# Latent up projection: rotary columns of q's weights held twice, rotation of raw values in two operations, k scaled by POOL

## The chip, the cores and the metric

The kernel runs on one core of one Trainium2 chip. A core has TensorE (PE, matrix products; PEld is its weight load), VectorE (DVE), ScalarE (ACT), GpSimd (POOL) and SyncE (SP), which issues the DMAs. Each engine works through its own queue in order; they meet at semaphores. The metric is the device time of one execution in microseconds.

## The reference

One layer of a streaming encoder, 1024 tokens of width 1024: a modulated RMS norm, one input projection, two groups of attention heads (latent attention "MLA" and chunk-band attention "CA"), an output projection, and a gated MLP with a short convolution. What matters here is the latent group, 8 heads of 64 plain and 32 rotary columns:

```python
def rope(x, positions):            # cut
    x1, x2 = xf[..., :half], xf[..., half:]
    out = jnp.concatenate([x1 * cos - x2 * sin, x2 * cos + x1 * sin], axis=-1)
...
q = jnp.dot(rmsnorm(q_lat, g_q_latent[l]), w_q_up[l]).reshape(B, S, MLA_HEADS, MLA_QK)
kv = jnp.dot(rmsnorm(kv_lat, g_kv_latent[l]), w_kv_up[l]).reshape(B, S, MLA_HEADS, MLA_NOPE + MLA_V)
k_nope, v = kv[..., :MLA_NOPE], kv[..., MLA_NOPE:]
k = jnp.concatenate([k_nope, jnp.broadcast_to(k_rope[:, :, None, :], (B, S, MLA_HEADS, MLA_ROPE))], axis=-1)
q = rmsnorm(q, g_mla_q[l])
k = rmsnorm(k, g_mla_k[l])
q = jnp.concatenate([q[..., :MLA_NOPE], rope(q[..., MLA_NOPE:], positions)], axis=-1)
k = jnp.concatenate([k[..., :MLA_NOPE], rope(k[..., MLA_NOPE:], positions)], axis=-1)
o_mla = mla_attention(q, k, v)
```

q is projected from a latent of rank 256, k and v from one of rank 128. Each head's q and k are divided by their root mean square over all 96 columns, and the last 32 columns are rotated by the token's position. The root mean square is one number for a token and head, so scaling and rotation can stand in either order.

## The kernel before, in words

Everything is computed with 128 tokens on the partitions. Products in 32 bits are made of a high and a low part of each operand: `gemm3` (L150) issues three matmuls for each pair, `hi_of` (L75) makes the high part on ACT, `lo_of` (L83) the rest on POOL or DVE.

The stages in order: modulation and norm (to about 70 us), input projection and chunk-band attention (to about 340 us), latent up projection (about 347 to 463 us), latent attention with the output projection of the other head group (to about 612 us), the rest of the output projection and the second norm (to about 710 us), then the MLP.

Attention and projections are woven together: `units` lists the attention units, each with four tiles of 128 queries; after the scores and values of each tile, `pace` takes steps from the list `fillers`, which holds the projections in a fixed order, among them `f_up(0)` and `f_up(1)`. A latent unit of head group 0 needs `f_up(0)` done; one of its second half of queries, `f_up(1)`, since `need` runs a filler to its end. `gemm3_f` yields a cost that depends on the columns of the product, and `pace` counts it.

The order of instructions on each engine is then planned by the framework: it simulates a timeline with modelled costs, scores, softmax and value products have a raised priority (`tc.high_priority`), and `tc.issue_after` pins some instructions behind others.

`f_up(gr)` (L628) handles one group of four heads. It loads q's weights (two pieces of 128 rows, 384 columns: 4 heads of 96) and the shared k and v weights (512 columns), splits them, and goes through the 8 token tiles. For each tile it

- projects q into a PSUM bank `qu` (L661), copies it to a row buffer `uqr` (L664, ACT), squares it (L666, ACT) and sums the squares by head (L669, DVE);
- projects k and v into `ku` (L671), copies k to `kraw` (L675), squares it (L677) and sums (L678); adds the sum of the shared rotary key (L679);
- makes both scales on POOL (`rsqrt_mean`, L119 and L120: a multiply-add and a power to -0.5);
- writes v as a high and a low half (`vt`, L682 on ACT, L683 on DVE);
- scales q into `qn` (L685, DVE) and rotates its rotary columns there with `rope_apply` (L497 to L500, four DVE operations, temporaries in the row buffer);
- scales k into `kn`: plain columns (L689) and the shared, already rotated key `kr` (L690), both on DVE.

Row buffers `uqr` and `kraw` come from one set of four (`rtile`). q and k are later transposed by PE (L729) into pages for the scores (L803). Softmax of a tile is a minimum on DVE (L822), an exponential on ACT (L829), the reciprocal on DVE (L831, L832), a scaling to 16 bits on POOL (L73), its residue on DVE (L851), and a transpose by DMA (L863) ahead of the value products (L891).

`rope_tables` (L539) makes cosine and sine tables times the norm's gains once, early: `tabq` for q and `tabk` for k, 64 columns each: 32 of cosine and 32 of sine (L611).

Of the kernel before, what the change touches and what calls it, by code (L numbers as in the profile page):

```python
# [18 lines left out]
AF = mybir.ActivationFunctionType  # L19
# [3 lines left out]
MUL, ADD, SUB, MIN, MAX = ALU.mult, ALU.add, ALU.subtract, ALU.min, ALU.max  # L23

P = 128
D = 1024
S = 1024
NT = S // P
# [5 lines left out]
QR, KVR, ROPE, NOPE, VD = 256, 128, 32, 64, 64  # L34
QK = NOPE + ROPE
# [29 lines left out]
def layer_kernel(ctx, tc, I, out):  # L65
    nc = tc.nc
    pe, act, dve, pool, sp = nc.tensor, nc.scalar, nc.vector, nc.gpsimd, nc.sync
# [7 lines left out]
    def hi_of(eng, o, i):  # L75
        if eng == "a":
            act.activation(o, i, AF.Copy)  # L77
        elif eng == "p":
            pool.tensor_scalar(o, i, 1.0, 0.0, op0=MUL, op1=ADD)
        else:  # L80
            dve.tensor_copy(o, i)

    def lo_of(eng, o, i, hi):  # L83
        (pool if eng == "p" else dve).tensor_tensor(o, i, f32(hi), op=SUB)  # L84
# [10 lines left out]
    pk = cst.tile([P, C_CV], F32, name="pk")  # L95
# [33 lines left out]
    tabq = apg.tile([P, NT, 64], F32, name="tabq")  # L129
# [409 lines left out]
    def rope_tables():  # L539
        cnt = [0]  # L540

        buf = [pgtile([P, 8, NT, 16], F32, f"rt{i}") for i in range(2)]

        def T():
            n = cnt[0] % 10
            cnt[0] += 1
            return buf[n // 8][:, n % 8]

        keep = (buf[1][:, 6], buf[1][:, 7])

        def rnd(src, q, o=None):
            o = T() if o is None else o
            dve.tensor_scalar(o, src, q, MAGIC, op0=MUL, op1=ADD)
            dve.tensor_scalar(o, o, MAGIC, None, op0=SUB)
            return o

        def fma(n, c, b):
            o = T()
            dve.scalar_tensor_tensor(o, n, c, b, op0=MUL, op1=ADD)
            return o  # L560

        p1 = _grid(TWO_PI, 2.0 ** -9)
        p2 = _grid(TWO_PI - p1, 2.0 ** -21)
        p3 = TWO_PI - p1 - p2

        def reduce(src):
            n = rnd(src, 1.0 / TWO_PI)
            yield
            r = fma(n, -p1, src)
            r = fma(n, -p2, r)  # L570
            yield
            return fma(n, -p3, r)

        pf = cst.tile([P, NT], F32, name="pf")
        dve.tensor_copy(pf[:], pos_i[:])
        ang = T()
        dve.tensor_tensor(ang, pf[:].unsqueeze(2).to_broadcast([P, NT, 16]),
                          pk[:, C_INV:C_INV + 16].unsqueeze(1).to_broadcast([P, NT, 16]), op=MUL)
        nh = rnd(ang, 2.0 ** -20, keep[0])
        rem = fma(nh, -(2.0 ** 20), ang)  # L580
        nm = rnd(rem, 2.0 ** -8, keep[1])
        lo = fma(nm, -(2.0 ** 8), rem)
        yield
        tot = yield from reduce(lo)
        for n, w in ((nh, 2.0 ** 20), (nm, 2.0 ** 8)):
            c = w - round(w / TWO_PI) * TWO_PI
            c1 = _grid(c, 2.0 ** -9)
            x = T()
            dve.tensor_scalar(x, n, c1, None, op0=MUL)
            yield  # L590
            x = fma(n, c - c1, (yield from reduce(x)))
            yield
            y = T()
            dve.tensor_tensor(y, tot, x, op=ADD)
            tot = y
        tot = yield from reduce(tot)
        yield
        pi_s = 3.1415925
        cl, cl2, sn, cn, c2 = buf[1][:, 2], buf[1][:, 3], buf[1][:, 4], buf[1][:, 5], T()
        dve.tensor_scalar(cl, tot, pi_s, -pi_s, op0=MIN, op1=MAX)  # L600
        dve.tensor_scalar(c2, tot, math.pi / 2, None, op0=ADD)
        yield
        dve.tensor_scalar(cl2, (yield from reduce(c2)), pi_s, -pi_s, op0=MIN, op1=MAX)
        act.activation(buf[1][:, 4:6], buf[1][:, 2:4], AF.Sin)
        yield

        for tab, c0 in ((tabq, C_RQ), (tabk, C_RK)):
            for half, trig in ((0, cn), (1, sn)):
                for j in range(2):
                    o = half * 32 + j * 16  # L610
                    dve.tensor_tensor(tab[:, :, o:o + 16], trig,  # L611
                                      pk[:, c0 + j * 16:c0 + j * 16 + 16].unsqueeze(1)
                                      .to_broadcast([P, NT, 16]), op=MUL)
                    yield

    rope = [None]
# [11 lines left out]
    def f_up(gr):  # L628
# [5 lines left out]
        wq = []  # L634
        for k in range(2):
            raw = qtile(f"wqr{gr}_{k}")
            sp.dma_start(raw[:, :384], I["w_qu"][gr][:, k, :])
            w = g4([P, 2, 512], F32R, f"wq{gr}_{k}")
            hi_of("a", w[:, 0, :384], raw[:, :384])
            lo_of("p", w[:, 1, :384], raw[:, :384], w[:, 0, :384])  # L640
            wq.append(w)
        raw = qtile(f"wkr{gr}")
        sp.dma_start(raw[:], I["w_kvu"][gr])
# [9 lines left out]
        for t in range(NT):  # L653
            h, j = divmod(t, 4)
            sl = slice(j * P, (j + 1) * P)
            if t % 2 == 0:
                mq[gr, t // 2] = g3([P, 2, 4, QK], F32, f"qn{gr}_{t}")
                mk[gr, t // 2] = g3([P, 2, 4, QK], F32, f"kn{gr}_{t}")
                mv[gr, t // 2] = G["v"].tile([P, 2, 4, 2, 64], F16, name=f"vt{gr}_{t}", tag="Gv", bufs=8)
            pt = ps.tile([P, 512], F32, name=f"qu{gr}_{t}", tag="mm", bufs=2)  # L660
            yield from gemm3_f(pt[:, :384], [(latT[k, h][:, 0, sl], latT[k, h][:, 1, sl], wq[k][:, 0, :384], wq[k][:, 1, :384])  # L661
                                for k in range(2)])
            rq = rtile(f"uqr{gr}_{t}")
            act.activation(rq[:, :384], pt[:, :384], AF.Copy)  # L664
            sq = qtile(f"usq{gr}_{t}")
            act.activation(sq[:, :384], rq[:, :384], AF.Square)  # L666
            ss = cst.tile([P, 8], F32, name=f"uss{gr}_{t}", tag="ss", bufs=4)
            r = cst.tile([P, 8], F32, name=f"ur{gr}_{t}", tag="rr", bufs=4)
            dve.tensor_reduce(ss[:, 0:4], sq[:, :384].rearrange("p (a b) -> p a b", a=4), axis=AX.X, op=ADD)  # L669
            pt = ps.tile([P, 512], F32, name=f"ku{gr}_{t}", tag="mm", bufs=2)  # L670
            yield from gemm3_f(pt[:], [(latT[2, h][:, 0, sl], latT[2, h][:, 1, sl], wk[:, 0], wk[:, 1])])  # L671
            p4 = pt[:].rearrange("p (a b) -> p a b", a=4)
            raw = rtile(f"kraw{gr}_{t}")
            r3 = raw[:, :256].rearrange("p (a b) -> p a b", a=4)
            act.activation(r3, p4[:, :, 0:NOPE], AF.Copy)  # L675
            s3 = raw[:, 256:512].rearrange("p (a b) -> p a b", a=4)
            act.activation(s3, r3, AF.Square)  # L677
            dve.tensor_reduce(ss[:, 4:8], s3, axis=AX.X, op=ADD)  # L678
            dve.tensor_tensor(ss[:, 4:8], ss[:, 4:8], ssr[:, t:t + 1].to_broadcast([P, 4]), op=ADD)  # L679
            rsqrt_mean(r[:], ss[:], QK)  # L680
            v_t = mv[gr, t // 2][:, t % 2]
            act.activation(v_t[:, :, 0, :], p4[:, :, NOPE:], AF.Copy, scale=sc)  # L682
            dve.scalar_tensor_tensor(v_t[:, :, 1, :], p4[:, :, NOPE:], sc, v_t[:, :, 0, :], op0=MUL, op1=SUB)  # L683
            q_t = mq[gr, t // 2][:, t % 2]
            dve.tensor_tensor(q_t, rq[:, :384].rearrange("p (a b) -> p a b", a=4),  # L685
                              r[:, 0:4].unsqueeze(2).to_broadcast([P, 4, QK]), op=MUL)
            rope_apply(q_t[:, :, NOPE:], q_t[:, :, NOPE:], tabq, t, 4, rq[:, 0:256], dve)
            k_t = mk[gr, t // 2][:, t % 2]
            dve.tensor_tensor(k_t[:, :, 0:NOPE], r3, r[:, 4:8].unsqueeze(2).to_broadcast([P, 4, NOPE]), op=MUL)  # L689
            dve.tensor_tensor(k_t[:, :, NOPE:], kr[:, t:t + 1, :].to_broadcast([P, 4, ROPE]),  # L690
                              r[:, 4:8].unsqueeze(2).to_broadcast([P, 4, ROPE]), op=MUL)


    def load_wo(k0, n, he, le):
# [887 lines left out]
def _inputs(a):  # L1582
# [11 lines left out]
    def rep(v):  # L1594
# [18 lines left out]
    ca = w_in[:, NM:].reshape(ND, P, 3, 4, 2, HD)  # L1613
    qk = ca[:, :, :2].transpose(3, 1, 0, 2, 4, 5).reshape(4, P, ND, 256)
    v = ca[:, :, 2].reshape(ND, P, 2, 256).transpose(2, 1, 0, 3)
    wa = f("w_ada")
    wa_a = np.stack([wa[:, D:2 * D], wa[:, :D]], 1).reshape(ND, P, 2, ND // 2, 2, P).transpose(3, 1, 0, 4, 2, 5)
    wa_a = wa_a.reshape(ND // 2, P, ND, 512)
# [2 lines left out]
        "x": a["x"][0], "w_ada": wa, "b_ada": a["b_ada"],  # L1621
        "bias": rb[:, idx],
        "w_qk": qk, "w_v": v, "w_ada_a": wa_a, "w_m": w_in[:, :NM].reshape(ND, P, NM).transpose(1, 0, 2),
        "w_qu": f("w_q_up").reshape(2, P, 2, 384).transpose(2, 1, 0, 3),
        "w_kvu": f("w_kv_up").reshape(P, 2, 512).transpose(1, 0, 2),
        "w_out": f("w_out"),
        "w_up": f("w_up").reshape(ND, P, 2 * NF, P).transpose(2, 1, 0, 3),
# [21 lines left out]
```

## Time and profile before

| what | value |
|---|---|
| median of 3 runs | 1333.23 us (1331.33 to 1334.52) |
| profiled execution, span from the first to the last instruction | 1332.7 us |
| PE busy | 1212.8 us, 91% |
| DVE busy | 1088.7 us, 82% |
| ACT busy | 622.3 us, 47% |
| POOL busy | 572.3 us, 43% |

The profiled execution is known by its span; it lies 0.5 us under the median of the runs. Busy time is a sum over engines that work beside one another, so the shares of the whole span are averages over stages with different limits. A row of a group of instructions gives line, engine, operation, the tiles written and read, the shape, the count, then busy microseconds, mean nanoseconds of one, and the idle time ahead of it with what ended it. A row by tile gives the minimum, the median and the maximum of one instruction.

### The profile page before, as it was taken

The numbers are of one execution on the slowest core, as the hardware profiler recorded it, in microseconds if no ns is written. First come the engines' busy times: TensorE is split into PE (matmuls) and PEld (weight loads), VectorE is DVE, ScalarE is ACT, GpSimd is POOL, SyncE is SP. The second block draws the span as 40 slices with busy tenths as digits, with TensorE's granted clock in tenths as the row PEclk, the third lists the DMA queues.
The fourth block names the chain that finished last, engine by engine and source line by source line (L and its number), as shares of the span: only waits on it lengthen the run. The fifth ranks groups of instructions, "written<-read, shape, count | busy, mean of one in ns | idle before, by whom it ended". The sixth has DMA issues, their size and how long they took to land.

```text
span 1332.7 us, 18710 instructions
## 1 busy us (share of the span) xinstructions
PE 1212.8 (91%) x6168; PEld 997.1 (75%) x6168; DVE 1088.7 (82%) x1928; ACT 622.3 (47%) x1132; POOL 572.3 (43%) x610
## 2 busy tenths in 40 slices
PE   3899999989667798888889999999999998999998
PEld 3888878868555576666677888888888886888886
DVE  6979898877589967894779888898889986687667
ACT  5454654445555545553366444444443444443331
POOL 5476773675675633354615445444444541000000
PEclk9899999989878798997999999999999998999999
DMA  8416768766123685879702333333333336943441
GB/s 321 144 55 156 164 143 197 150 151 138 35 72 70 119 172 122 152 164 326 275 16 79 106 124 111 122 116 108 113 106 132 111 119 221 393 151 114 132 159 63
DMA packets 223689, 190.57 MB, mean 143 GB/s; under 512 B 148708, under 2 KB 166884, under 8 KB 223592
## 3 DMA queue, kind: packets, MB, share of 16 engines
q1 hardware_dynamic: 223592, 189.38, 50.3%
q8 instruction: 48, 0.79, 0.3%
q14 instruction: 49, 0.40, 0.1%
HBM read 117.24 MB, written 37.49 MB: 116 GB/s over the span
## 4 chain that ended last, share of the span: by engine, by line
PE 48%; DVE 3%; DMA 2%; issue 1%; ACT 1%; POOL 0%; SPq 0%; POOLq 0%; DVEq 0%
PE p L1125 10%; PE p L1126 10%; PE p L1127 10%; PE dnA_P L1460 2%; PE dnA_P L1461 2%; PE dnA_P L1462 2%; PE dnB_P L1461 1%; PE dnB_P L1460 1%; PE dnB_P L1462 1%; PE dnA L1461 1%; PE dnA L1460 1%; PE dnA L1462 1%; PE dnB L1461 1%; PE dnB L1462 1%; PE dnB L1460 1%
## 5 line engine op out<-in xcount | busy, mean ns | idle before, releaser
L77 ACT ACTIVATE dnP<-dnr 128x1024 fp32r<-128x1024 f32 x73 | 77.4, 1064 | 117.5 <-PE dnA_P L1462 46.4
L1434 DVE TENSOR_TENSOR dnP<-dnr,dnP 128x1024 fp32r<-128x1024 f32 x72 | 87.9, 1224 | 52.7 <-ACT dnP L77 47.7
L73 POOL TENSOR_SCALAR hlm<-Pm,rim 128x512 f16<-128x512 f32 (+2 forms) x96 | 65.4, 691 | 77.5 <-DVE rim L832 32.0
L84 POOL TENSOR_TENSOR wf<-wu,wf 128x512 fp32r<-128x512 f32 x22 | 39.8, 1808 | 118.2 <-ACT wf L77 118.2
L1296 DVE SCALAR_TENSOR_TENSOR u<-c,cvp,u 128x1023 f32<-128x1023 f32 x44 | 58.6, 1372 | 27.8 <-ACT u L1295 27.8
L84 POOL TENSOR_TENSOR wb<-wu,wb 128x512 fp32r<-128x512 f32 x22 | 42.2, 1920 | 75.0 <-ACT wb L77 59.6
L73 POOL TENSOR_SCALAR hlc<-Pc,ric 128x640 f16<-128x640 f32 (+2 forms) x64 | 48.0, 753 | 54.5 <-DVE ric L832 25.8
L851 DVE SCALAR_TENSOR_TENSOR hlm<-Pm,rim,hlm 128x512 f16<-128x512 f32 (+2 forms) x96 | 65.9, 696 | 5.5 <-POOL hlm L73 5.2
L829 ACT ACTIVATE Pc<-sc,mc 128x640 f32<-128x640 f32 (+2 forms) x64 | 42.2, 660 | 55.2 <-DVE mc L818 26.1
L891 PE MATMUL pvm<-PTm,vt 128*128 128x256 f16 (+1 forms) x320 | 47.7, 302 | 22.1 <-DMA PTm<-hlm 14.2
L829 ACT ACTIVATE Pm<-sm,mm 128x128 f32<-128x128 f32 (+3 forms) x64 | 47.1, 738 | 37.7 <-DVE mm L822 21.2
L1295 ACT ACTIVATE u<-c,cvp 128x1024 f32<-128x1024 f32 x44 | 52.4, 1238 | 26.0 <-DVE c L1394 18.0
L1297 DVE SCALAR_TENSOR_TENSOR u<-c,cvp,u 128x1022 f32<-128x1022 f32 x44 | 61.7, 1442 | 0.0
L891 PEld LDWEIGHTS <-vt 128*128 128x128 f16 x320 | 33.1, 111 | 37.0 <-issue 21.6
L77 ACT ACTIVATE wc<-ws 128x512 fp32r<-128x512 f32 x21 | 13.3, 632 | 91.9 <-DVE ws L1144 86.1
L154 PE MATMUL ipq<-wq_s,hT 128*128 128x256 f32 x192 | 55.7, 290 | 0.0
L156 PE MATMUL ipq<-wq_s,hT 128*128 128x256 f32 x192 | 55.4, 288 | 0.0
L155 PE MATMUL ipq<-wq_s,hT 128*128 128x256 f32 x192 | 55.1, 287 | 0.0
L851 DVE SCALAR_TENSOR_TENSOR hlc<-Pc,ric,hlc 128x640 f16<-128x640 f32 (+2 forms) x64 | 49.2, 774 | 6.8 <-POOL hlc L73 6.7
L1461 PE MATMUL dnA_P<-dnP 128*128 128x512 f32 x132 | 51.3, 389 | 0.0
L1462 PE MATMUL dnA_P<-dnP 128*128 128x512 f32 x132 | 51.3, 389 | 0.0
L1460 PE MATMUL dnA_P<-dnP 128*128 128x512 f32 x132 | 51.2, 389 | 0.0
(442 smaller groups left out, 4413.7 us busy)
## 6 DMA issues: line engine op xcount, KB each, us to landing
wu<-w_up SPq DMA_DIRECT2D x44, 512.0 KB, 3.5
dnr<-g_d SPq DMA_DIRECT2D x73, 256.0 KB, 2.8
aw<-w_ada SPq DMA_DIRECT2D x48, 256.0 KB, 3.4
g_d<-u SPq DMA_DIRECT2D x22, 512.0 KB, 3.0
dnr<-w_down SPq DMA_DIRECT2D x44, 256.0 KB, 5.4
adaw<-w_ada_a SPq DMA_DIRECT2D x16, 512.0 KB, 6.0
x<-x SPq DMA_DIRECT2D x16, 512.0 KB, 9.8
g_d<-gs SPq DMA_DIRECT2D x22, 256.0 KB, 2.8
```

The costliest lines, as they stand in the source:

```text
L73: pool.tensor_scalar(o, i, s, 1.0, op0=MUL, op1=MUL)
L77: act.activation(o, i, AF.Copy)
L84: (pool if eng == "p" else dve).tensor_tensor(o, i, f32(hi), op=SUB)
L829: act.activation(pr[:, :n], sv, AF.Exp, bias=m[:], scale=-1.0, accum_out=rsum[:, 0:1])
L851: dve.scalar_tensor_tensor(hl[:, w:2 * w], pp, ri[:], hl[:, :w], op0=MUL, op1=SUB)
L1125: pe.matmul(pt, sh, pg[:, 0], start=(k == 0 and not add), stop=False, skip_group_check=skip)
L1126: pe.matmul(pt, sh, pg[:, 1], start=False, stop=False, skip_group_check=skip)
L1127: last = pe.matmul(pt, sl, pg[:, 0], start=False, stop=(k == 3), skip_group_check=skip)
L1434: r = f(*a, **k)
L1460: pe.matmul(pt, sh, w[:, 0, 0], start=start, stop=False, skip_group_check=add)
L1461: pe.matmul(pt, sh, w[:, 1, 0], start=False, stop=False, skip_group_check=add)
L1462: pe.matmul(pt, sl, w[:, 0, 0], start=False, stop=stop, skip_group_check=add)
```

## The change

Host side, the weights of q get 32 more columns for each head: the rotary columns once more with their halves swapped, so a head has 64 + 32 + 32 = 128 columns and a group 512. The projection then yields, for each head, the raw rotary values and the same values swapped. The table for q holds the sine half in swapped order, with a minus sign for its first 16 columns. The rotation is one product of the 64 columns (32 and 32 swapped) with the table, in place in the row buffer, and one sum of the two halves. Both stand ahead of the scaling, right behind the sum of squares. The squares are taken of the first 96 columns of each head. The scaling L685 then reads the first 96 columns of each head and writes `qn`. The four operations of `rope_apply` go for q. The two scalings of k move from DVE to POOL.

```diff
@@ rope_tables
-                    dve.tensor_tensor(tab[:, :, o:o + 16], trig,
-                                      pk[:, c0 + j * 16:c0 + j * 16 + 16].unsqueeze(1)
-                                      .to_broadcast([P, NT, 16]), op=MUL)
+                    swap = half == 1 and tab is tabq
+                    g0 = c0 + (1 - j if swap else j) * 16
+                    dve.scalar_tensor_tensor(tab[:, :, o:o + 16], trig, -1.0 if swap and j == 0 else 1.0,
+                                             pk[:, g0:g0 + 16].unsqueeze(1).to_broadcast([P, NT, 16]),
+                                             op0=MUL, op1=MUL)
@@ f_up, weights
-            sp.dma_start(raw[:, :384], I["w_qu"][gr][:, k, :])
+            sp.dma_start(raw[:], I["w_qu"][gr][:, k, :])
             w = g4([P, 2, 512], F32R, f"wq{gr}_{k}")
-            hi_of("a", w[:, 0, :384], raw[:, :384])
-            lo_of("p", w[:, 1, :384], raw[:, :384], w[:, 0, :384])
+            hi_of("a", w[:, 0], raw[:])
+            lo_of("p", w[:, 1], raw[:], w[:, 0])
@@ f_up, each token tile
-            yield from gemm3_f(pt[:, :384], [(latT[k, h][:, 0, sl], latT[k, h][:, 1, sl], wq[k][:, 0, :384], wq[k][:, 1, :384])
+            yield from gemm3_f(pt[:], [(latT[k, h][:, 0, sl], latT[k, h][:, 1, sl], wq[k][:, 0], wq[k][:, 1])
                                 for k in range(2)])
             rq = rtile(f"uqr{gr}_{t}")
-            act.activation(rq[:, :384], pt[:, :384], AF.Copy)
+            act.activation(rq[:], pt[:], AF.Copy)
+            rq4 = rq[:].rearrange("p (a b) -> p a b", a=4)
             sq = qtile(f"usq{gr}_{t}")
-            act.activation(sq[:, :384], rq[:, :384], AF.Square)
+            act.activation(sq[:, :384].rearrange("p (a b) -> p a b", a=4), rq4[:, :, :QK], AF.Square)
...
             dve.tensor_reduce(ss[:, 0:4], sq[:, :384].rearrange("p (a b) -> p a b", a=4), axis=AX.X, op=ADD)
+            dve.tensor_tensor(rq4[:, :, NOPE:], rq4[:, :, NOPE:],
+                              tabq[:, t:t + 1, :].to_broadcast([P, 4, 64]), op=MUL)
+            dve.tensor_tensor(rq4[:, :, NOPE:QK], rq4[:, :, NOPE:QK], rq4[:, :, QK:], op=ADD)
...
-            dve.tensor_tensor(q_t, rq[:, :384].rearrange("p (a b) -> p a b", a=4),
-                              r[:, 0:4].unsqueeze(2).to_broadcast([P, 4, QK]), op=MUL)
-            rope_apply(q_t[:, :, NOPE:], q_t[:, :, NOPE:], tabq, t, 4, rq[:, 0:256], dve)
+            dve.tensor_tensor(q_t, rq4[:, :, :QK], r[:, 0:4].unsqueeze(2).to_broadcast([P, 4, QK]), op=MUL)
             k_t = mk[gr, t // 2][:, t % 2]
-            dve.tensor_tensor(k_t[:, :, 0:NOPE], r3, r[:, 4:8].unsqueeze(2).to_broadcast([P, 4, NOPE]), op=MUL)
-            dve.tensor_tensor(k_t[:, :, NOPE:], kr[:, t:t + 1, :].to_broadcast([P, 4, ROPE]),
-                              r[:, 4:8].unsqueeze(2).to_broadcast([P, 4, ROPE]), op=MUL)
+            pool.tensor_tensor(k_t[:, :, 0:NOPE], r3, r[:, 4:8].unsqueeze(2).to_broadcast([P, 4, NOPE]), op=MUL)
+            pool.tensor_tensor(k_t[:, :, NOPE:], kr[:, t:t + 1, :].to_broadcast([P, 4, ROPE]),
+                               r[:, 4:8].unsqueeze(2).to_broadcast([P, 4, ROPE]), op=MUL)
@@ _inputs
+    qu = f("w_q_up").reshape(2, P, 2, 4, QK)
+    qu = np.concatenate([qu, qu[..., NOPE + 16:], qu[..., NOPE:NOPE + 16]], axis=-1)
...
-        "w_qu": f("w_q_up").reshape(2, P, 2, 384).transpose(2, 1, 0, 3),
+        "w_qu": qu.reshape(2, P, 2, 512).transpose(2, 1, 0, 3),
```

## The prediction

> **What bounds the kernel now.** I read the page's head first, then the chain that ended last, then busy time by stretches around the latent up projection, then the groups of DVE and the waits in those stretches.
>
> ```profile
> span 1332.7 us, 18710 instructions
> ...
> 598.03 0.48 DVE hlm L851
> ...
> 347.00:384.00 37.00, 25.19 (x102) 18.34 (x102) 30.55 (x107) 21.70 (x55) 19.83 (x22) 0.87 0.08 20
> 384.00:463.00 79.00, 59.36 (x271) 45.70 (x272) 71.48 (x210) 42.27 (x99) 50.44 (x53) 0.80 0.46 95
> 463.00:600.00 137.00, 119.67 (x681) 95.13 (x679) 109.83 (x275) 69.95 (x148) 57.10 (x78) 0.96 0.75 151
> 347.00:463.00 116.00, 84.55 (x372) 64.04 (x373) 102.03 (x316) 63.98 (x152) 70.27 (x74) 0.82 0.33 71
> ```
>
> The second line is the earliest entry of the chain: it reaches back only to 598 us, so it says nothing of the place that is changed, and the stretches have to. Their columns are the stretch, its length, then PE, weight loads, DVE, ACT and POOL busy, the granted clock, the DMA share and GB/s. The up projection of both head groups runs from 347 to 463 us: group 0 nearly alone up to 384, group 1 mixed with the first latent attention tiles. DVE is the fullest engine there, 102.0 of 116 us (88%), and 71.5 of 79 (90%) in the mixed part; PE has 84.6, POOL 70.3. From 463 to 600, when only attention and its output projection are left, PE has 119.7 of 137 (87%). So what shortens DVE's list before 463 should let the attention, which can use no more than is projected, start sooner; the end follows as far as PE and POOL let it.
>
> The groups of DVE in 347 to 463 us that the change touches (busy, mean ns):
>
> ```profile
> L685 DVE TENSOR_TENSOR qn<-uqr,ur 128x384 f32<-128x384 f32 x16 | 10.7, 670 | 0.4 <-POOL ur L120 0.3
> ...
> L689 DVE TENSOR_TENSOR kn<-kraw,ur 128x256 f32<-128x256 f32 x16 | 8.5, 530 | 0.0
> ...
> L499 DVE TENSOR_TENSOR qn<-uqr 128x64 f32<-128x64 f32 x16 | 5.4, 336 | 0.1
> ...
> L498 DVE TENSOR_TENSOR uqr<-qn,tabq 128x128 f32<-128x128 f32 x16 | 4.9, 305 | 0.0
> L497 DVE TENSOR_TENSOR uqr<-qn,tabq 128x128 f32<-128x128 f32 x16 | 4.9, 304 | 0.0
> L500 DVE TENSOR_TENSOR qn<-uqr 128x64 f32<-128x64 f32 x16 | 4.8, 299 | 0.0
> L690 DVE TENSOR_TENSOR kn<-kr,ur 128x128 f32<-128x128 f32 x16 | 4.7, 292 | 0.0
> ```
>
> And the waits of the same stretch that hang on them (total, times, longest):
>
> ```profile
> POOL uss L119 <- DVE uss L679: 23.8, 11, 4.1
> ...
> ACT uqr L664 <- DVE kn L689: 8.4, 8, 1.4
> ...
> ACT kraw L675 <- DVE qn L500: 7.7, 4, 2.8
> PEld mq_ps L729 <- DVE qn L500: 7.3, 3, 3.1
> ```
>
> POOL waits for sums that DVE makes late; ACT waits for row buffers that DVE's k scaling and rotation hold; PE waits for rotated q. All four point at DVE's queue.
>
> **The change, part by part.** Durations (min/median/max) for what is removed, added or widened, from the views by tile and by line:
>
> ```profile
> L689 DVE TENSOR_TENSOR kn<-kraw,ur x16: 402/418/1496, 355.7 to 457.5; 128x256 f32<-128x256 f32 x16
> L690 DVE TENSOR_TENSOR kn<-kr,ur x16: 273/282/371, 356.1 to 458.2; 128x128 f32<-128x128 f32 x16
> ```
>
> *DVE loses* the four rotation operations and the two k operations in each of 16 tiles: 5.4 + 4.9 + 4.9 + 4.8 + 8.5 + 4.7 = 33.2 us by the groups above. *DVE gains* per tile one 128x256 product (table times raw rotary values) and one 128x128 sum of the same kinds as the two rows just shown: 16 x (0.418 + 0.282) = 11.2 us. L685 stays. Net -22.0 us of DVE. The new pair stands behind the reduction L669, which already waits for ACT's square, so it adds no wait; L679 of the tile and the softmax operations queue behind it as they did behind the rotation.
>
> *POOL gains* the two k operations. The trace has none of them on POOL; the nearest rows:
>
> ```profile
> L356 POOL TENSOR_TENSOR qn<-raw,r x12: 1034/1044/1619, 118.4 to 277.9; 128x512 f32<-128x512 f32 x12
> L84 POOL TENSOR_TENSOR wq_s<-wq_r,wq_s x32: 722/749/1385, 25.3 to 199.4; 128x256 fp32r<-128x256 f32 x32
> L120 POOL TENSOR_TENSOR ur<-uss,nhalf x16: 1633/1640/2165, 353.6 to 455.1; 128x8 f32<-128x8 f32 x16
> ```
>
> L356 is the same operation with the same broadcast scale over 512 columns; by columns it gives 0.52 + 0.26 = 0.78 us a tile as the lower bound, and 384 columns at L84's 0.75 us for 256 give 1.1 us as the upper one. I take 1.0, since a fixed part is paid twice: 16 us, bounds 12.5 to 18. They follow the power L120 on its own queue, so they wait for nothing new; behind them wait the next L119 and softmax scalings L73. POOL goes from 70.3 to some 87 us in a stretch of 116.
>
> *What two engines do to one another* is the open price. Here is the trace at 384 us, in order of time:
>
> ```profile
> 384.86 1.29 POOL L84 TENSOR_TENSOR wk<-wkr,wk 128x512 fp32r<-128x512 f32 x1
> 384.93 1.63 DVE L685 TENSOR_TENSOR qn<-uqr,ur 128x384 f32<-128x384 f32 x1
> ...
> 386.10 1.60 POOL L84 TENSOR_TENSOR wo<-wor,wo 128x512 fp32r<-128x512 f32 x1
> ...
> 386.49 1.50 DVE L689 TENSOR_TENSOR kn<-kraw,ur 128x256 f32<-128x256 f32 x1
> ...
> 356.97 1.64 POOL L120 TENSOR_TENSOR ur<-uss,nhalf 128x8 f32<-128x8 f32 x1
> 357.00 0.24 DVE L500 TENSOR_TENSOR qn<-uqr 128x64 f32<-128x64 f32 x1
> ```
>
> L685 has a mean of 0.67 and took 1.63 beside a POOL subtraction; k's L689 (median 0.418) took 1.50 beside the next one. Products of two SBUF tensors on the two engines stand in each other's way. The power L120 doesn't: L500 took 0.24 inside it, which is less than its mean of 0.30. In the new order POOL's k product and DVE's q product L685 are both released by the same L120, so they meet. Lower bound: nothing, where DVE reaches L685 late. Upper bound: both k operations, 1.1 us a tile, 18 us in all. A gain below nothing: fewer DVE products would free POOL's own scalings; I have no row for that and count none. I take the first k operation alone, 0.6 us (a little over half of L356), since the pair at 386 us shows DVE getting its turn between two POOL operations: 16 x 0.6 = 9.6 us. DVE's net is then -22.0 + 9.6 = -12.4 us, with bounds -22 and -4.
>
> The Trainium skill says of this ("SBUF — State Buffer", section on the two separate sides) that GpSimd and a VectorE operation with two SBUF inputs share a port pair, and that whoever starts first holds it for the whole instruction. The L84 rows agree; the L120 row doesn't, for there the wide side ran on. By the rule to the letter DVE would meet every k operation, which is the upper bound.
>
> *PE* works on q's weights 512 columns wide in place of 384; *ACT* copies 512 columns; the weights' residue on POOL and their loads widen; the tables are made by a three-input form:
>
> ```profile
> L155 PE MATMUL qu<-wq,latT x32: 335/336/522, 348.5 to 437.0; 128*128 128x384 f32 x32
> L155 PE MATMUL ku<-wk,latT x16: 392/397/776, 350.5 to 442.4; 128*128 128x512 f32 x16
> L664 ACT ACTIVATE uqr<-qu x16: 476/491/492, 350.3 to 441.6; 128x384 f32<-128x384 f32 x16
> L349 ACT ACTIVATE raw<-ipq x12: 581/598/601, 111.8 to 264.9; 128x512 f32<-128x512 f32 x12
> L84 POOL TENSOR_TENSOR wq<-wqr,wq x4: 992/997/1023, 342.4 to 380.7; 128x384 fp32r<-128x384 f32 x4
> L84 POOL TENSOR_TENSOR wk<-wkr,wk x2: 1267/1277/1287, 347.3 to 384.9; 128x512 fp32r<-128x512 f32 x2
> DMA to landing us min/median/max: 2.4/2.6/2.9
> L559 DVE SCALAR_TENSOR_TENSOR rt<-rt,rt x6: 276/282/662, 98.5 to 140.8; 128x128 f32<-128x128 f32 x6
> L611 DVE TENSOR_TENSOR tabq<-rt,pk x4: 282/288/293, 147.3 to 149.3; 128x128 f32<-128x128 f32 x4
> ```
>
> PE: 96 matmuls x (0.397 - 0.336) = +5.9 us. The cover is PE's idle time in the stretch, 116 - 84.6 = 31 us; if DVE no longer supplies that cover the 5.9 are paid. ACT: 16 x 0.107 = 1.7 us at an engine with 64 of 116. POOL: 4 x 0.28 = 1.1 us ahead of each group's first tile, hidden behind the last latent pages and DVE's backlog; 0.6 a group if not. The four weight loads grow by a third at a landing time of 2.6 us, issued long before use; SP issues as many as before. Tables: 8 x nothing (0.282 against 0.288). The row buffer of q is freed at L685 in place of L500, about a microsecond sooner (0.30 + 0.30 + 0.34 + 0.30 less overlap), which takes most of ACT's 7.7 us wait; next to be late is the power chain on POOL.
>
> **The sum.** DVE -12.4 us, of which I let half reach the end, because PE at 84.6 + 5.9 and POOL at 87 are then as full as DVE at 90: -6.2 us. 1332.7 - 6.2 = 1326.5 on the profiled execution; the median shown is 0.5 above that span, so 1327.0.
>
> **The rivals.**
> *Everything arrives:* DVE comes to L685 late, meets nothing, and 22.0 us shrink by its share of 88% less a little of PE's growth: about -16, 1317. For it: L685 waited 0.4 us in all for its scale, so DVE was the late one. Against it: 5.9 us more of PE.
> *The collisions eat it (no change):* the upper bound of 1.1 us on each tile leaves DVE -4, half of it at the end, 1331. For it: the 1.63 and 1.50 above; against it the turn in between.
> *POOL's queue becomes the bound (slower):* in the mixed part each tile puts 1.0 to 1.1 us of k work, and its waits for DVE's products, ahead of softmax scalings, which release the residue on DVE and the transposes by DMA. With 8 tiles and 1.1 us each this is +8.8, 1342. It decides when POOL's idle time there, 79 - 50.4 = 28.6 us, does not shrink, that is when the 23.8 us of L119 behind L679 stay although DVE has less ahead of L679. For it: that wait is the longest of all; against it: its cause is the very queue that is shortened. The instruction order is planned from modelled costs, and another order of DVE and POOL would show up as this case too.
>
> **How the numbers follow.** The forecast (1327, its own range 1322 to 1330) has 0.42, everything arriving 0.15, no change 0.14, slower 0.29. Within 0.2% means within 2.7 us of 1333.2, about what a measurement of this kernel can tell. Faster is 0.42 + 0.15 = 0.57, same 0.14, slower 0.29. The range takes in the cases on both sides, 1316 to 1343, and leaves out a tenth above and less below.
>
> **What would show it.** Right: DVE busy in the up projection falls by 10 to 20 us, L685's mean rises to about 1.0 us, POOL's wait for L679 falls well under 23.8 us, the last score of latent attention comes some 6 us sooner than at 598 us, and everything behind 600 us takes as long as before. Wrong: POOL's k operations at 1.5 us and more, L73 with a higher mean, DVE idle behind POOL, or the same end of the stretch with PE at 95%. A change behind 600 us would mean that something I left out moved.

## The result, and the profile after

The changed kernel takes 1326.2 us (median; 1322.65 to 1333.59) against 1332.36 us of the kernel before on the same chips (1329.29 to 1338.85). The ratio is 0.9954, with a 95% interval of 0.9941 to 0.9966: faster by 0.46%, about 6 us. The forecast was 1327.0.

The profiled execution of the changed kernel has a span of 1331.8 us, hardly less than the 1332.7 before. That is no contradiction. Up to the up projection both kernels have the same order of instructions, and yet this execution is already late there. The first matmul of the first q projection, in the timeline of the kernel before and then of the changed kernel (start, duration, engine and line):

```profile
348.04 0.67 PE L154 MATMUL qu<-wq,latT 128*128 128x384 f32 x1
```

```profile
352.34 0.77 PE L154 MATMUL qu<-wq,latT 128*128 128x512 f32 x1
```

4.3 us of lateness came before the changed part begins. So stages are compared from mark to mark and not by the clock of the execution, and a second profile of the changed kernel stands beside the first.

Busy time by stretches of the changed kernel (columns as in the prediction: PE, weight loads, DVE, ACT, POOL, granted clock, DMA share, GB/s):

```profile
347.00:384.00 37.00, 27.50 (x105) 18.79 (x105) 26.95 (x80) 21.55 (x53) 26.56 (x33) 0.87 0.09 26
384.00:463.00 79.00, 59.48 (x275) 44.96 (x276) 69.91 (x175) 45.55 (x104) 70.78 (x76) 0.79 0.45 100
463.00:600.00 137.00, 117.48 (x676) 94.36 (x675) 108.57 (x272) 69.33 (x145) 58.71 (x76) 0.96 0.71 147
347.00:463.00 116.00, 86.97 (x380) 63.74 (x381) 96.86 (x253) 67.09 (x157) 97.34 (x108) 0.82 0.33 76
```

In the up projection DVE falls from 102.0 to 96.9 us, and POOL rises from 70.3 to 97.3: POOL is now as full as DVE. In the mixed part POOL has 70.8 of 79 us and DVE still has 69.9. The fixed window cuts the work of the two kernels at different places, so here is the same stage by its own marks, from the first q projection to the last write into the score tiles of latent attention (the mask of the last one, L821 before). First the kernel before, then the changed kernel, then its second profile:

```profile
348.00:597.70 249.70, 202.48 (x1041) 157.65 (x1042) 209.97 (x584) 133.58 (x297) 126.25 (x150) 0.90 0.56 115
```

```profile
352.30:599.10 246.80, 201.31 (x1035) 155.44 (x1036) 203.28 (x520) 134.08 (x296) 152.91 (x182) 0.90 0.54 115
```

```profile
349.30:592.70 243.40, 198.78 (x1036) 153.40 (x1037) 202.40 (x520) 134.17 (x296) 151.04 (x181) 0.91 0.56 117
```

DVE runs 64 instructions fewer (584 to 520), four a tile, and is busy 6.7 or 7.6 us less. POOL is busy 25 to 27 us more. The stage is 2.9 or 6.3 us shorter.

The forecast of 12.4 us less can't be held against that busy time as it stands, for it was added up from rows, and the records of DVE overlap. From the timeline of the kernel before:

```profile
355.26 0.55 DVE L685 TENSOR_TENSOR qn<-uqr,ur 128x384 f32<-128x384 f32 x1
...
355.73 0.42 DVE L689 TENSOR_TENSOR kn<-kraw,ur 128x256 f32<-128x256 f32 x1
356.07 0.29 DVE L690 TENSOR_TENSOR kn<-kr,ur 128x128 f32<-128x128 f32 x1
...
356.27 0.16 DVE L679 TENSOR_TENSOR uss<-uss,ssr 128x4 f32<-128x4 f32 x1
```

Each record begins a little before the one ahead of it ends. k's two operations are 0.71 us by their records, but only 0.54 us from the start of the first to the start of what follows (356.27 - 355.73). A sum of rows counts the overlaps twice, the engine's busy time counts them once. By the sum of its rows over the stage, DVE has 241.9 us in the first profile before and 241.0 in a second, and 229.2 and 228.7 in the two after: 12.5 us less on average, just what was forecast. As busy time that is only some 7 us.

The groups of DVE in 347 to 463 us after, of the instructions that the change adds or touches:

```profile
L691 DVE TENSOR_TENSOR qn<-uqr,ur 128x384 f32<-128x384 f32 x16 | 10.8, 676 | 0.8 <-POOL ur L120 0.8
...
L673 DVE TENSOR_TENSOR uqr<-uqr,tabq 128x256 f32<-128x256 f32 x16 | 7.4, 461 | 0.0
...
L675 DVE TENSOR_TENSOR uqr<-uqr 128x128 f32<-128x128 f32 x16 | 6.2, 386 | 0.0
...
L685 DVE TENSOR_TENSOR uss<-uss,ssr 128x4 f32<-128x4 f32 x16 | 5.0, 314 | 0.0
```

The last of them, which adds the shared key's sum of squares for four heads, had this row before (L679 there):

```profile
L679 DVE TENSOR_TENSOR uss<-uss,ssr 128x4 f32<-128x4 f32 x16 | 2.4, 149 | 0.1
```

L691 is the q product (L685 before), which the forecast had as the place of collision: its mean is 676 ns, against 670 before. The rotation's product (L673) costs 461 ns, priced 418; its sum (L675) 386, priced 282; and the addition of four columns (L685) has doubled. One group that the change doesn't touch is dearer too, the softmax residue; its row over the whole stage, before and then after:

```profile
L851 DVE SCALAR_TENSOR_TENSOR hlm<-Pm,rim,hlm 128x512 f16<-128x512 f32 (+2 forms) x91 | 61.9, 690 | 4.2 <-POOL hlm L73 4.0
```

```profile
L855 DVE SCALAR_TENSOR_TENSOR hlm<-Pm,rim,hlm 128x512 f16<-128x512 f32 (+3 forms) x91 | 66.8, 742 | 13.0 <-POOL hlm L73 12.7
```

The same operations (91 records each) take 4.9 us more, and DVE stands idle 12.7 us in place of 4.0 ahead of them, waiting for POOL's scaling. POOL's two new operations and its multiply-add, in 347 to 463 us again:

```profile
L693 POOL TENSOR_TENSOR kn<-kraw,ur 128x256 f32<-128x256 f32 x16 | 13.2, 823 | 0.9
...
L694 POOL TENSOR_TENSOR kn<-kr,ur 128x128 f32<-128x128 f32 x16 | 9.6, 600 | 0.0
...
L119 POOL TENSOR_SCALAR uss<-uss 128x8 f32<-128x8 f32 x16 | 4.0, 250 | 9.9 <-DVE uss L685 7.3 <-DVE rim L836 1.5
```

They cost 22.8 us, priced 16 with an upper bound of 18. The timeline of the changed kernel shows who stops whom in one token tile:

```profile
364.43 0.55 DVE L691 TENSOR_TENSOR qn<-uqr,ur 128x384 f32<-128x384 f32 x1
364.44 1.01 POOL L693 TENSOR_TENSOR kn<-kraw,ur 128x256 f32<-128x256 f32 x1
364.89 0.70 DVE L675 TENSOR_TENSOR uqr<-uqr 128x128 f32<-128x128 f32 x1
...
365.42 0.44 POOL L694 TENSOR_TENSOR kn<-kr,ur 128x128 f32<-128x128 f32 x1
...
365.52 0.35 DVE L685 TENSOR_TENSOR uss<-uss,ssr 128x4 f32<-128x4 f32 x1
...
367.96 0.61 POOL L693 TENSOR_TENSOR kn<-kraw,ur 128x256 f32<-128x256 f32 x1
```

Both engines are released by the power L120 at the same moment. DVE is first and takes its usual 0.55 us; POOL's product waits for it (1.01 in place of the 0.61 that it takes at 367.96, where it starts first); DVE's next operation then waits until POOL's product is over (0.70 in place of 0.28), and the next but one waits for k's second product. So where the two meet, POOL pays for it, and then the small operations of DVE behind the q product. This agrees with the Trainium skill ("SBUF — State Buffer", section on the two separate sides): whoever starts first holds the shared ports for the whole instruction and the other is blocked. In most tiles the q product keeps its usual time: its median over the 16 tiles is 554 ns, while POOL's first product has a median of 686.

The waits of the stretch after (total, times, longest):

```profile
POOL uss L119 <- DVE uss L685: 7.3, 4, 5.4
ACT uqr L666 <- POOL kn L693: 7.0, 5, 1.9
...
PEld mq_ps L733 <- DVE qn L691: 4.9, 6, 1.4
...
ACT kraw L681 <- POOL kn L693: 3.6, 2, 2.0
...
ACT uqr L666 <- DVE qn L691: 1.9, 3, 1.2
```

POOL's wait for the sum of squares fell from 23.8 to 7.3 us. Of ACT's two waits for a row buffer, the one for q's rows fell from 7.7 us (behind L500) to 1.9 (behind L691). The one for k's raw rows changed hands: 8.4 us behind DVE's L689 before, 10.6 (7.0 + 3.6) behind POOL's product now.

### The profile page after: what moved, and what is told of

It is laid out like the page before. It is cut to its first block, busy times and chain, and to the rows that moved or that the text cites. A ratio compares the mean times of both kernels' runs of the same rounds, so it can differ in the third digit from the quotient of the medians.

```text
span 1331.8 us, 18692 instructions
## 1 busy us (share of the span) xinstructions
PE 1211.5 (91%) x6168; PEld 994.7 (75%) x6168; DVE 1086.8 (82%) x1864; ACT 623.0 (47%) x1132; POOL 603.2 (45%) x642
## 4 chain that ended last, share of the span: by engine, by line
PE 41%; DVE 8%; issue 2%; ACT 2%; POOL 1%; DMA 1%; SPq 0%; DVEq 0%; ACTq 0%; POOLq 0%
PE p L1129 7%; PE p L1131 7%; PE p L1130 7%; PE dnA_P L1464 2%; PE dnA_P L1466 2%; PE dnA_P L1465 2%; PE dnB_P L1466 1%; PE dnB_P L1464 1%; PE dnB_P L1465 1%; DVE u L1301 1%; DVE u L1300 1%; PE op L154 1%; PE dnA L1465 1%; PE dnA L1464 1%; PE op L155 1%
## 5 line engine op out<-in xcount | busy, mean ns | idle before, releaser
L73 POOL TENSOR_SCALAR hlm<-Pm,rim 128x512 f16<-128x512 f32 (+3 forms) x96 | 68.6, 725 | 74.2 <-DVE rim L836 19.9
L855 DVE SCALAR_TENSOR_TENSOR hlm<-Pm,rim,hlm 128x512 f16<-128x512 f32 (+3 forms) x96 | 70.8, 745 | 14.5 <-POOL hlm L73 14.2
L895 PE MATMUL pvm<-PTm,vt 128*128 128x256 f16 (+1 forms) x320 | 45.8, 291 | 31.5 <-DMA PTm<-hlm 20.6
L895 PEld LDWEIGHTS <-vt 128*128 128x128 f16 x320 | 31.8, 107 | 46.3 <-issue 23.8
L155 PE MATMUL ipq<-wq_s,hT 128*128 128x256 f32 x192 | 55.4, 288 | 0.0
```

Of the source, the lines that this page charges most:

```text
L73: pool.tensor_scalar(o, i, s, 1.0, op0=MUL, op1=MUL)
L855: dve.scalar_tensor_tensor(hl[:, w:2 * w], pp, ri[:], hl[:, :w], op0=MUL, op1=SUB)
```

## The experiments

Ratios are to the kernel before on the same chip, with 95% intervals; a ratio need not be the quotient of the two medians given beside it. A stage runs between the marks named above, in one profile.

**The two kernels again.** Neither is edited.

> The changed kernel as it stands, for a second profile and a time on the same chip as the parts. Theory (DVE's list in the up projection is shortened, half of it reaches the end): about 6 us under the kernel before, and from the first q projection to the first product of the MLP this profile is 3 to 6 us shorter than the one of before, while the stretch ahead of the first q projection is as long as before within run-to-run noise. Rival (the gain is a matter of the planned order behind 600 us): the last score is as late as before, counted from the first q projection, and the difference arises between the first output-projection product and the first product of the MLP.

> The kernel before once more under a label of its own, for the size of the noise and a second profile. Every theory: ratio 1.000 within 0.002; its profile tells how far the marks of two executions of one kernel lie apart, ahead of the up projection and behind it: I expect up to 4 us.

The changed kernel came to 0.9954 (0.9937 to 0.9971; 1327.63 against 1334.99 us) once more, and the kernel before to 0.999 (0.997 to 1.001). So the 0.46% stands. The second profile of the kernel before shows what a single profile is worth:

```profile
347.70:593.80 246.10, 200.79 (x1041) 156.34 (x1042) 209.30 (x584) 133.28 (x297) 129.64 (x150) 0.90 0.56 117
```

The stage is 246.1 us here and 249.7 in the first profile, with the same instructions. The means of two each are 247.9 before and 245.1 after: the lengths of the stage don't show a gain of 6 us. POOL has 129.6 us here, so that it is busy 21 to 23 us more after, against this profile. A longer stretch shows more. The planned orders of the two kernels differ from the first q projection to the first product into `p` of the MLP (its rows are shown below, under the second norm); ahead of it and behind it they are the same. This stretch takes 351.3 and 351.2 us in the two profiles before, and 347.3 and 343.9 in the two after: 5.6 us less on average.

**The rotation alone.** k goes back to DVE; the wide weights and the rotation in two operations stay. Against the changed kernel:

```diff
-            pool.tensor_tensor(k_t[:, :, 0:NOPE], r3, ...)
-            pool.tensor_tensor(k_t[:, :, NOPE:], kr[:, t:t + 1, :]...)
+            dve.tensor_tensor(k_t[:, :, 0:NOPE], r3, ...)
+            dve.tensor_tensor(k_t[:, :, NOPE:], kr[:, t:t + 1, :]...)
```

> The rotation in two operations alone: wide q weights, product and sum ahead of the scaling, but k scaled by DVE as before. Theory: DVE loses 20.0 us of the four operations and gains 11.2, net 8.8, half of it at the end: 4.4 us under the kernel before, about 1328, that is 2 us slower than the whole change. Rival (the move of k to POOL is a loss that the rotation pays for): 8 to 10 us under the kernel before, 1322 to 1324, faster than the whole change. Rival (the move of k makes the gain): no change against before, within 3 us.

Measured 0.9959 (0.9939 to 0.9979), 1328.06 us: not to be told from the whole change. The stage, two groups of DVE and POOL's wait:

```profile
348.50:594.30 245.80, 198.27 (x1035) 152.38 (x1036) 204.61 (x551) 134.25 (x296) 132.19 (x149) 0.91 0.56 116
```

```profile
L675 DVE TENSOR_TENSOR uqr<-uqr 128x128 f32<-128x128 f32 x16 | 4.5, 279 | 0.0
...
L685 DVE TENSOR_TENSOR uss<-uss,ssr 128x4 f32<-128x4 f32 x16 | 2.8, 172 | 0.0
```

```profile
POOL uss L119 <- DVE uss L685: 26.3, 9, 5.7
```

Three readings. The rotation's part takes DVE's busy time from 210.0 to 204.6 us, and the sum of its rows from 241.9 to 234.2. Moving k's operations, 13.2 us of rows, takes that sum only on to 229.2 or 228.7: some 8 of the 13.2 us come back as longer operations elsewhere on DVE, and its busy time falls on by 1.3 or 2.2 us. With k on DVE the rotation's sum and the addition cost 279 and 172 ns, so it is k on POOL that makes them 386 and 314. And POOL's wait stays at 26.3 us with 5 us less on DVE, while with k on POOL alone (the next experiment) it is 9.1: in the changed kernel it fell because POOL's own k products fill that time, not because DVE is earlier.

**k on POOL alone,** in the kernel before, with its narrow weights and four-operation rotation (the two `dve` of L689 and L690 become `pool`).

> The kernel before with k scaled by POOL and nothing else. Theory: DVE loses 13.2 us and pays 9.6 in collisions, net 3.6, half of it at the end: about 2 us under the kernel before, 1330.5. Rival (POOL's queue is the bound once k is on it): 4 to 9 us slower than before, 1336 to 1341, with POOL's softmax scalings later. Rival (the move of k makes the gain): 6 us under the kernel before, 1326.

Measured 1.0012 (0.9995 to 1.0029), 1335.81 us: no gain, between what theory and rival have. Its stage, and DVE's second rotation product (304 and 305 ns for the two before) and last rotation sum (299 before):

```profile
347.90:601.50 253.60, 199.28 (x1040) 155.25 (x1041) 209.38 (x551) 132.98 (x295) 146.48 (x182) 0.90 0.54 111
```

```profile
L498 DVE TENSOR_TENSOR uqr<-qn,tabq 128x128 f32<-128x128 f32 x15 | 6.7, 445 | 0.0
...
L500 DVE TENSOR_TENSOR qn<-uqr 128x64 f32<-128x64 f32 x15 | 6.1, 408 | 0.0
```

13.2 us of rows were taken off DVE (584 to 551 instructions in the records). The sum of its rows is 237.6 us instead of 241.9, so some 9 of them came back, and it is busy 209.4 us instead of 210.0. Moving this work to POOL is next to no relief for DVE.

**The width alone.** The wide weights and their copy stay, the added columns are used by nothing, and the rotation is again four operations behind the scaling; k is on DVE. Against the changed kernel, beside k's lines as above:

```diff
-                    swap = half == 1 and tab is tabq
+                    swap = False
...
-            dve.tensor_tensor(rq4[:, :, NOPE:], rq4[:, :, NOPE:], tabq..., op=MUL)
-            dve.tensor_tensor(rq4[:, :, NOPE:QK], rq4[:, :, NOPE:QK], rq4[:, :, QK:], op=ADD)
...
+            rope_apply(q_t[:, :, NOPE:], q_t[:, :, NOPE:], tabq, t, 4, rq[:, 0:256], dve)
```

> The kernel before with q's weights and its row buffers 512 columns wide, the added columns projected and copied but used by nothing; rotation in four operations on scaled values and k on DVE, as before. It prices the width alone. Theory: 5.9 us of PE and 1.7 us of ACT beside a DVE that is the fullest engine: 0 to 2 us slower, 1332.5 to 1334.5. Rival (PE is as much the bound as DVE): the whole 5.9 us, 1338.

Measured 0.9962 (0.9944 to 0.9981), 1328.91 us. Its stage:

```profile
349.40:599.40 250.00, 205.18 (x1047) 157.52 (x1047) 215.72 (x584) 135.29 (x296) 131.78 (x150) 0.90 0.54 114
```

This kernel only adds work, is busier on DVE (215.7 us for 210.0) and PE (205.2 for 202.5), and is as much faster as the whole change, which neither theory has. A shorter list of DVE can't be its reason. What it shares with the others is that the instructions are ordered anew: the q projection reports a larger cost to `pace`, and the planner has wider products to place. Ahead of the first q projection and behind the first product into `p` the orders of all these kernels are the same, between these they differ.

**The reported cost alone.** The kernel before, where the q projection reports the cost of 512 columns and everything computed stays the same:

```diff
-    def gemm3_f(pt, pairs, step=GSTEP):
-        n, w = len(pairs), pt.shape[-1]
+    def gemm3_f(pt, pairs, step=GSTEP, w=None):
+        n, w = len(pairs), w or pt.shape[-1]
...
-                                for k in range(2)])
+                                for k in range(2)], w=512)
```

> The kernel before, with one number changed: the q projection reports to the pacing the cost of 512 columns in place of 384 (975 becomes 1295 for a token tile). No instruction is added, removed or widened; only how the up projection's steps are woven between attention tiles, and what the planner makes of it. Theory of work (what DVE, PE and POOL have to do decides): the same as before, within 2 us. Rival (the gain of 5 us that width alone brought is the weaving, since the wide product reports more cost): 3 to 6 us under the kernel before.

Measured 0.997 (0.995 to 0.999), 1330.35 against 1333.73 us. One number that costs no instruction brings 0.3%, though only just clear of noise: the kernel before, run again on the same chip, has an interval of 0.997 to 1.001.

**The other way round:** the width alone, the rotation alone and the whole change with the cost of 384 columns reported (`w=384` at the same place).

> Width alone, with the pacing told 384 columns as before. Theory of weaving: the 5 us of width alone go, and the added 5.9 us of PE and 1.7 us of ACT are left: as before or up to 3 us slower than it. Rival (wide matmuls help by themselves, by a planner that expects the q projection later or a clock that is granted more): still 4 to 6 us under the kernel before.

> Rotation in two operations, k on DVE, pacing told 384 columns. With the pacing of 512 the move of k to POOL was worth nothing (0.9954 with, 0.9959 without). Theory (k's move gains 13 us of DVE and loses nearly all of it to collisions): within 2 us of the changed kernel under the same pacing, 0.992 to 0.995. Rival (the move is worth several us and the pacing of 512 hid it): 0.996.

> The changed kernel with the pacing told 384 columns as before: rotation in two operations and k on POOL, but the weaving steps costed as they were. Theory of weaving: the gain is lost, 0 to 2 us under the kernel before. Theory of work (DVE's shorter list): still 5 to 6 us under the kernel before.

> The changed kernel under the pacing of 384 once more, with a second profile, on the same chip as the three others. If 0.992 was the order and not the run: 0.991 to 0.994 again, with 240 to 243 us from the first q projection to the last score.

The width alone came out as its rival has it. The other two fit neither of their theories: the rotation lost its gain, the whole change gained more. The repeat confirms the latter.

All results together, ratio to the kernel before:

| edit | 384 columns reported | 512 columns reported |
|---|---|---|
| none | 1 (again: 0.999, 0.997 to 1.001) | 0.997 (0.995 to 0.999) |
| width alone | 0.996 (0.9943 to 0.9976) | 0.9962 (0.9944 to 0.9981) |
| width and rotation | 1.0004 (0.9982 to 1.0026) | 0.9959 (0.9939 to 0.9979) |
| k on POOL alone | 1.0012 (0.9995 to 1.0029) | not run |
| whole change | 0.992 (0.9892 to 0.9948); again 0.9924 (0.9901 to 0.9947) | 0.9954 (0.9941 to 0.9966) |

The parts don't add up. In the left column the width brings 0.4%, the width with the rotation nothing, k on POOL alone nothing, and all of them together 0.8%; in the right column the step from the rotation to the whole change is worth nothing. The same rotation is worth 0.4% or nothing by a number that only orders, and these two intervals don't meet. Each edit draws a new order of the stretch from 340 to 700 us, and the draws differ by 0.3 to 0.4%, as much as the change itself. For the width alone the reported cost makes no difference; whether its 0.4% come from the order that is planned for wide products or from the products themselves, no run separates. The whole change with 384 columns reported is the lowest twice, though its intervals still meet those of the others. Its stage in the second run's profile:

```profile
348.60:589.80 241.20, 198.98 (x1035) 152.96 (x1036) 204.40 (x519) 133.02 (x295) 147.46 (x181) 0.91 0.56 119
```

241.2 us, some 4 less than the mean of the changed kernel, with DVE and PE as busy as there. What makes this order better than the others is not settled.

**Row buffers.** In the changed kernel ACT's copies of q wait for POOL to give a row free. Here k's raw rows get three buffers of 256 columns of their own, in the whole change with 384 columns reported:

```diff
-            raw = rtile(f"kraw{gr}_{t}")
-            r3 = raw[:, :256].rearrange("p (a b) -> p a b", a=4)
+            raw = rtile(f"ksq{gr}_{t}")
+            kraw = G["k"].tile([P, 256], F32, name=f"kraw{gr}_{t}", tag="Gk", bufs=3)
+            r3 = kraw[:].rearrange("p (a b) -> p a b", a=4)
```

> The changed kernel under the pacing of 384, with three buffers of 256 columns of its own for k's raw rows; only k's squares and q's rows share the four row buffers. In the profile after, the first head group's tiles still came every 3.55 us, as before, though DVE has less to do. Theory (the four row buffers set that period: each new q row waits for k's release two tiles back): under 3.2 us a tile, 2 to 3 us in all sooner at the first score of the second half, 0.990 to 0.992 overall. Rival (POOL's queue sets it, 0.2 + 1.64 + 0.82 + 0.60 us a tile): the period stays at 3.3 to 3.55 and the time as without it.

Measured 0.9915 (0.989 to 0.9939), 1321.59 us: the fastest kernel here, and a version that beats both. Of the eight copies of q of head group 0, the first, one in the middle and the last in the timeline, first of the changed kernel, then of this one (the bracket is the idle time before, and what ended it):

```profile
355.29 0.60 ACT L666 ACTIVATE uqr<-qu 128x512 f32<-128x512 f32 x1 [2.30 <-PE qu L156]
...
368.61 0.60 ACT L666 ACTIVATE uqr<-qu 128x512 f32<-128x512 f32 x1 [1.17 <-POOL kn L693]
...
379.40 0.60 ACT L666 ACTIVATE uqr<-qu 128x512 f32<-128x512 f32 x1 [1.07 <-POOL kn L693]
```

```profile
351.73 0.60 ACT L666 ACTIVATE uqr<-qu 128x512 f32<-128x512 f32 x1 [2.30 <-PE qu L156]
...
362.52 0.60 ACT L666 ACTIVATE uqr<-qu 128x512 f32<-128x512 f32 x1 [0.29 <-PE qu L156]
...
372.35 0.60 ACT L666 ACTIVATE uqr<-qu 128x512 f32<-128x512 f32 x1 [0.54 <-PE mk_ps L734]
```

In the changed kernel the eight copies take 24.1 us from first to last, 3.44 us a tile, and five of them wait for rows; with rows enough they take 20.6 us, 2.95 a tile, and wait for PE. (With 384 columns reported and the shared rows the period is 3.45 too.) So the row buffers set a part of the period of head group 0, about 0.5 us a tile, as the theory has it. It is worth little at the end: the stage is 239.2 us against 241.2, and 0.9915 can't be told from 0.992 and 0.9924.

**The second norm.** In the kernel before, the profile shows a gap behind 660 us that the changed kernel doesn't have, from the place of one scaling (L1193) in DVE's order. Timeline of the kernel before:

```profile
665.03 3.46 DVE L1193 TENSOR_SCALAR x<-x,r 128x1024 f32<-128x1024 f32 x2
...
668.42 2.28 DVE L1186 TENSOR_TENSOR x<-x,pa 128x1024 f32<-128x1024 f32 x1
...
671.35 0.50 PE L1126 MATMUL c_g<-b,wa 128*128 128x512 f32 x1 [2.52 <-DVE b L84]
```

The first product into `c_g` and the first into `p` of the MLP mark the stage; rows by tile (min, median, max, first start to last end), before and then after:

```profile
L1125 PE MATMUL c_g<-b,wa x8: 393/400/628, 664.2 to 696.5; 128*128 128x512 f32 x8
...
L1125 PE MATMUL p<-b,wa x84: 394/396/399, 699.3 to 1088.9; 128*128 128x512 f32 x84
```

```profile
L1129 PE MATMUL c_g<-b,wa x8: 393/396/496, 667.7 to 696.8; 128*128 128x512 f32 x8
...
L1129 PE MATMUL p<-b,wa x84: 394/396/399, 699.6 to 1089.1; 128*128 128x512 f32 x84
```

From the one to the other there are 35.1 us before (699.3 - 664.2) and 31.9 after. The experiment moves the scaling of token tile 6 behind the sum L1186 of tile 7 and the residue of a first page (`page1`), and leaves the up projection alone:

```diff
-        dve.tensor_tensor(x1[:], x1[:], pa[:], op=ADD)
+        added = dve.tensor_tensor(x1[:], x1[:], pa[:], op=ADD)
...
+        if t == 7:
+            with tc.issue_after(added.ins), tc.issue_after(page1):
+                dve.tensor_scalar(xn2[6][:], xn2[6][:], r2[:, 6:7], 1.0, op0=MUL, op1=MUL)
...
-        dve.tensor_scalar(x1[:], x1[:], r2[:, t:t + 1], 1.0, op0=MUL, op1=MUL)
+        if t != 6:
+            dve.tensor_scalar(x1[:], x1[:], r2[:, t:t + 1], 1.0, op0=MUL, op1=MUL)
```

> The kernel before with one move behind the attention: the second norm's scaling of token tile 6 stands on DVE behind the last residual sum and the first page's residue, where the changed kernel has it, instead of ahead of both. The up projection is untouched, instruction for instruction. Every variant so far, the one that changes only a number of the pacing among them, has 3.2 us less than the kernel before between the first product of the MLP's first tile and the first of its second part (31.9 against 35.1). Theory (that is the late order's doing, an accident of the plan): this kernel gets the 3.2 us, ratio about 0.9975, and PE's wait of 2.5 us for the residue goes. Rival (those 3.2 us come down from the attention's earlier end): 35 us there as before, ratio 1.000.

The same two rows with the scaling moved:

```profile
L1125 PE MATMUL c_g<-b,wa x8: 391/396/496, 662.6 to 691.7; 128*128 128x512 f32 x8
...
L1125 PE MATMUL p<-b,wa x84: 394/396/399, 694.5 to 1084.0; 128*128 128x512 f32 x84
```

694.5 - 662.6 = 31.9 us: the gap is gone in the profile. The time is 1.0003 (0.9985 to 1.0022), 1332.93 against 1333.53 us: no gain, where 3.2 us would be 0.9976. So the gap in the norm doesn't explain the result, and why closing it isn't seen in the time stays open. This profile is also a warning: its stretch from the first q projection (348.9) to the first product into `p` is 345.6 us, as short as the changed kernel's, in a kernel that is no faster.

## Why the prediction was right or wrong

The number was right: 1326.2 us against 1327.0, inside the likeliest case's own range. That is luck in good part: of the working only some terms held, and the step from DVE's shorter list to the end isn't shown.

- *DVE loses 33.2 us and gains 11.2: right as rows, not as time.* The instructions are as listed. The two new ones cost 13.6 us, 7.4 + 6.2, mostly because the sum meets POOL. But the records of DVE overlap, so the rows overstate what the engine is relieved of. Its busy time falls by 6.7 or 7.6 us over the stage and from 102.0 to 96.9 in the fixed window; the sign "falls by 10 to 20 us" did not come.
- *Collisions, 9.6 us at the q product: right in size, at the wrong place.* The sum of DVE's rows falls by 12.5 us where -22.0 + 9.6 = -12.4 was forecast, so some 9.5 us came back. None of it is at the q product, whose mean is 676 ns and not about 1.0 us. It is the residue of the softmax (+4.9), the addition of four columns (L685 after; +2.6), the rotation's sum (+1.7, 16 x 0.104) and its product (+0.7). Half of the residue's part comes with k on DVE as well (64.5 us by the rotation alone, against 61.9 and 66.8), so that half isn't owed to k. That the size agrees is luck: it was priced as one meeting of k's first product in each tile.
- *POOL, 16 us with bounds of 12.5 to 18: wrong, 22.8.* The price without a meeting was right: at their shortest the two take 0.609 and 0.393 us, 1.0 a tile. The term that failed is that collisions were charged to DVE alone. POOL rose to 97 us and not to 87.
- *PE and ACT hidden:* right. q's copies went from 0.49 to 0.60 us and its matmuls from a median of 0.336 to 0.394 (L155), as priced, and PE is no busier in the stage (202.5 before; 201.3 and 198.8 after). PE has 29 of the 116 us idle, 31 before.
- *Row buffers freed sooner:* right for q's rows, for which ACT waits 1.9 us in place of 7.7. Left out was that k's rows are held longer by the slower product on POOL: 10.6 us of waits in place of 8.4.
- *POOL's wait for the sum of squares well under 23.8 us:* it is 7.3, but the sign was read wrongly. With DVE's list shortened and k still on DVE the wait is 26.3. It fell because POOL works in that time, so it was no test of POOL's queue as the bound. A sign of the wrong case, DVE idle behind POOL, did come: 12.7 us ahead of the residue in place of 4.0. The kernel is faster all the same, so the slower case did not come.
- *Half of DVE's gain reaches the end:* not shown. Half of the fall in DVE's busy time would be 3.5 us; the time fell by 6. The width alone, with more work on DVE, brings the same, and a number that only re-orders brings 0.3%. So the time can't be put down to DVE's list. The forecast named another order only as something that could turn the case to slower; it is at least as likely a part of the gain.
- *Behind 600 us as before:* wrong in the profile, 31.9 for 35.1 us in the norm, by the order and not by the work; in the time, moving that scaling alone shows nothing.

What stays open: what share of the 6 us is the change itself and what share its order. With 384 columns reported the whole change brings 0.8%, twice, and of its parts one brings 0.4% and two nothing; the runs give no mechanism for it.

## What to carry to other kernels

A product of two SBUF tensors that is moved from DVE to POOL should be priced as hardly any relief where DVE runs such products at the same time: here 8 to 9 of 13.2 us of rows came back on DVE, its busy time fell by 0.6 us in one kernel and 1.3 to 2.2 in another, and POOL paid 22.8. Where an engine's records overlap, don't hold a sum of rows against its busy time: compare sums with sums. Where a planner orders the instructions, run a neutral edit that changes only its costs before a gain of half a per cent is put down to the work that was saved. A wait that shrinks on an engine that was given more work says nothing about its cause.

## What the runs showed of the hardware

The first q projection starts between 346.2 and 352.3 us over the fourteen profiles of these kernels, though the instructions ahead of it stand in the same order. One profile can't show a difference of 6 us in the span; the interval over many runs can. And on POOL the same k product takes 0.61 us at its shortest and 0.82 on average (1.39 at most) in the changed kernel: the price of a move between these two engines is not read from either engine's rows alone.
